# Grouped-query heads of an encoder layer: the scores of two heads issued in one step, instead of one head per step

## The chip, the cores and the metric

The kernel runs on one core of a Trainium2 chip. The metric is the device time of one execution in microseconds (us). The engines are TensorE (PE; its weight loads are a lane of their own, PEld), VectorE (DVE), ScalarE (ACT), GpSimd (POOL) and SyncE (SP, which issues the DMAs). Matmuls write to PSUM, and DVE and ACT read from there.

## The reference

Two pre-norm residual layers over 1024 tokens with 1024 channels. The change lies in the first layer's mixer, in its second half:

```python
# A: differential attention, 4 heads x 2 score maps, v of 128 columns
# B: grouped-query attention, 8 query heads of 64, 2 key/value heads
def gqa_attention(q, k, v):            # q (b,s,2,4,64), k and v (b,s,2,64)
    scale = HEAD_DIM ** -0.5
    def block(qb):                     # 128 queries against all 1024 keys
        s = jnp.einsum('bqgrd,bkgd->bgrqk', qb, k).astype(jnp.float32) * scale
        pr = jax.nn.softmax(s, axis=-1).astype(v.dtype)
        return jnp.einsum('bgrqk,bkgd->bqgrd', pr, v)
    return from_blocks(lax.map(block, to_blocks(q)))
```

The rest (differential attention, neighbourhood attention, the gated ConvFFN, the input embedding, the norms) stays as it is.

## The kernel before

**Precision.** Each float32 operand is split into a high part and a low part of a narrower matmul type, and a product is the sum of three matmuls. For scores the 64 channels of a head fill only half of the 128 rows, so the high and the low part of q are stacked on the 128 rows: one full matmul of 128 rows (line 964, `qs` against `ks`, with the high part of k on both halves) gives two of the three products, and one matmul of 64 rows (line 969, the high half of `qs` against the low part `kl`) gives the third. For heads with even index the high part lies in the lower half of the rows, for odd ones in the upper half (`own`). Scores of 128 queries against 1024 keys fill a PSUM tile S of two banks, so a head needs two matmuls of each kind. There are two S tiles in rotation (`psS`, `bufs=2`), and four more PSUM tiles of one bank each, called b (`psb`), which all other steps share in rotation.

**Work items.** `its` lists 96 items in order: 0 to 31 are (unit, query block) of A, where one item holds both score maps; 32 to 95 are (unit, query block, head j) of B, with 2 units, 8 query blocks, and 4 heads each. An item passes through these stages:

- `qk(n)`: the scores on PE, then the negated row maximum on DVE (line 972).
- `exp(n)`: ACT takes the exponential of S with the row sum as a by-product (line 981), which is issued as two instructions, the activation and a read of the accumulator; the S tile is free after the second.
- `tr(n)`: PE transposes P in two groups of four (line 1007) into two b tiles, and ACT copies each as the high part (line 1017); `tr2(n)`: DVE subtracts to get the low part (line 1029), after which the b tile is free.
- `pv(n)`, for odd j only: 16 matmuls against v for both heads (line 1044); `tail_a`: an ACT copy and a DVE add (lines 1061, 1062); `tail_b`: two small transposes and a DVE multiply (lines 1073, 1078); `place_b`, once in four items: two transposes, an ACT copy and a DVE subtraction (lines 1090, 1093, 1094).

**Order.** Each engine runs its instructions in the order in which the program issues them, so the order in `step(n)` is the order on every queue. For an item of B, step n issues `qk(n)`, `tr(n-2)`, `exp(n)`, `tr2(n-2)`, then `pv(n-3)`, `tail_b(n-4)`, `tail_a(n-3)` and `place_b(n-5)`. So `pv` and `place_b` come in even steps, `tail_b` in odd steps. Between the two halves of a step the main loop puts in other work by hand-written lists of step numbers: one block of the input projection (24 matmuls of 384 columns) at the steps of `PROJ5` (of those from 32 on: 33, 35, 37), one block of the output projection (12 matmuls of 512 columns, lines 175 to 177, and a DVE addition, line 258) at the steps of `GEMM` (57, 59, 61, 63, then every third from 67 to 100), and DVE work left over from the step before (`later`). At the end of a step come the transposes that finish unit 5's queries and keys (`FIN5`: 49, 51, ... 59), those of A's result (`PLACE`: even steps 40 to 54), and a split of the next weight tile (line 164 on ACT, 165 on DVE) where there is room for one.

In A, where an item has two score maps, the same `qk` issues four full matmuls and then four of 64 rows, in the order lower, upper, lower, upper half. In B it issues two full ones and then two of 64 rows, both in the same half:

```python
            for hk in halves:
                for b, ps in zip(bs, e["S"]):
                    o = own[b % 2]
                    nc.tensor.matmul(ps[:, hk], qs[b][o, qc], kl[o, hk], start=False, stop=True)
```

Of the kernel before, what the change touches and what calls it, by code (L numbers as in the profile page):

```python
# [25 lines left out]
P = 128  # L26
S = 1024
# [79 lines left out]
class Kern:  # L107
# [657 lines left out]
    def even(self, W, ready, load, after):  # L765
# [29 lines left out]
        def background(n):  # L795
            while bg and n > 0:
                bg.popleft()()
                n -= 1
# [149 lines left out]
        L, MS = {}, {}  # L948

        def qk(n):  # L950
            u, qt, j = its[n]
            A = u < 4
            if A and qt == 0:
                M[u] = self.u([P, NT, P], F32, "mix")
            qs, ks, kl = st[u]["q"], st[u]["k"], st[u]["kl"]
            e = L[n] = {"P": [], "nm": [], "S": []}
            e["s"] = self.col(2) if j % 2 == 0 else L[n - 1]["s"]
            bs = (0, 1) if A else (j,)
            qc = slice(qt * P, (qt + 1) * P)
            halves = (slice(0, 512), slice(512, 1024))  # L960
            for b in bs:
                ps = self.tS()
                for hk in halves:
                    nc.tensor.matmul(ps[:, hk], qs[b][:, qc], ks[b % 2][:, hk], start=True, stop=False)
                e["S"].append(ps)
# [4 lines that stand above are left out]
            for ps in e["S"]:  # L970
                nm = self.col()
                nc.vector.tensor_reduce(nm, ps, axis=AX.X, op=ALU.max, negate=True)  # L972
                e["nm"].append(nm)

        def exp(n):
            u, qt, j = its[n]
            e = L[n]
            for b, (ps, nm) in enumerate(zip(e.pop("S"), e.pop("nm"))):
                p = self.u([P, S], F32, "P")
                c = b if u < 4 else j % 2  # L980
                nc.scalar.activation(p, ps, AF.Exp, bias=nm, accum_out=e["s"][:, c:c + 1])  # L981
                e["P"].append(p)

        def combine(n):
            u, qt, j = its[n]
            e = L[n]
            if u < 4:
                r = e["r"] = self.col(3)
                s0 = e["s"][:, 0:1]
                nc.vector.reciprocal(r[:, 0:2], e["s"])  # L990
                nc.vector.scalar_tensor_tensor(r[:, 2:3], s0, nlam, r[:, 1:2], op0=ALU.mult, op1=ALU.mult)
                nc.vector.scalar_tensor_tensor(e["P"][0], e["P"][1], r[:, 2:3], e["P"][0],
                                               op0=ALU.mult, op1=ALU.add)
            elif j % 2 == 1:
                r = e["r"] = self.col(2)
                nc.vector.reciprocal(r, e["s"])

        def tr(n):
            u, qt, j = its[n]
            e = L[n]  # L1000
            w = e.pop("P")[0]
            e["T"] = []
            for h in range(2):
                ps = self.tb()
                for b in range(4):
                    kt = 4 * h + b
                    nc.tensor.transpose(ps[:, b * P:(b + 1) * P], w[:, kt * P:(kt + 1) * P], self.ident)
                e["T"].append(ps.rearrange("p (b c) -> p b c", b=4))
            if u < 4:
                e["pt"] = self.u([P, NT, P], F32, "pt")  # L1010
            else:
                if j % 2 == 0:
                    e["pt"] = [[self.u([P, 4, 2, P], F32R, "pt") for _ in range(2)] for _ in range(2)]
                else:
                    e["pt"] = L[n - 1]["pt"]
                for h in range(2):
                    nc.scalar.copy(e["pt"][h][0][:, :, j % 2], e["T"][h])

        def tr2(n):
            u, qt, j = its[n]  # L1020
            e = L[n]
            T = e.pop("T")
            if u < 4:
                nc.scalar.copy(e["pt"][:, 0:4, :], T[0])
                nc.vector.tensor_copy(e["pt"][:, 4:8, :], T[1])
            else:
                for h in range(2):
                    hi, lo = e["pt"][h]
                    nc.vector.tensor_sub(lo[:, :, j % 2], T[h], hi[:, :, j % 2].bitcast(F32))

        def pv(n):
            u, qt, j = its[n]
            e = L[n]
            v = st[u]["v"]
            if u < 4:
                o = e["o"] = self.tb()
                for kt in range(NT):
                    nc.tensor.matmul(o[:, :P], e["pt"][:, kt, :], v[:, kt, :], start=(kt == 0), stop=(kt == NT - 1))
                e.pop("pt")
            elif j % 2 == 1:  # L1040
                o = e["o"] = self.tb()
                for kt in range(NT):
                    for x in range(2):
                        nc.tensor.matmul(o[:, :256], v[:, kt, :], e["pt"][kt // 4][x][:, kt % 4].rearrange("p a b -> p (a b)"),
                                         start=(kt + x == 0), stop=(kt == NT - 1 and x == 1))
                e.pop("pt")
                L[n - 1].pop("pt")

        def tail_a(n):
            u, qt, j = its[n]  # L1050
            e = L[n]
            if u < 4:
                os = e["os"] = self.os()
                ss = self.col()
                xo = M[u][:, qt, :]
                nc.scalar.activation(os[:, :P], e["o"][:, :P], AF.Copy, scale=e["r"][:, 0:1])
                nc.scalar.activation(xo, os[:, :P], AF.Square, accum_out=ss)
                e["rs"] = self.rstd(ss, 1.0 / P)
            elif j % 2 == 1:
                os = e["os"] = self.os()  # L1060
                nc.scalar.copy(os[0:64], e["o"][64:128, :256])
                nc.vector.tensor_add(os[0:64], e["o"][0:64, :256], os[0:64])

        def tail_b(n):
            u, qt, j = its[n]
            e = L[n]
            if u < 4:
                xo = M[u][:, qt, :]
                nc.vector.scalar_tensor_tensor(xo, e["os"][:, :P], e["rs"], gs, op0=ALU.mult, op1=ALU.mult)
            elif j % 2 == 1:  # L1070
                ps = self.tb()
                for b in range(2):
                    nc.tensor.transpose(ps[:, b * 64:b * 64 + 64], e["os"][0:64, b * P:(b + 1) * P],
                                        self.ident[0:64, 0:64])
                if j == 1:
                    MS[u, qt] = self.os()
                xo = MS[u, qt][:, (j // 2) * P:(j // 2 + 1) * P].rearrange("p (h d) -> p h d", h=2)
                nc.vector.tensor_mul(xo, ps[:, :P].rearrange("p (h d) -> p h d", h=2),
                                     e["r"][:, :, None].to_broadcast([P, 2, 64]))
            L.pop(n)  # L1080

        its = [(u, qt, j) for u in range(6) for qt in range(NT) for j in range(1 if u < 4 else 4)]
        N = len(its)
# [17 lines left out]
        def place_b(n):  # L1101
            u, qt, j = its[n]
            ms = MS.pop((u, qt))
            place([ms[:, :P], ms[:, P:]], 2 * u - 4, qt)

        def step(n):

            A = lambda m: 0 <= m < 32
            B = lambda m: 32 <= m < N
            if n < N:  # L1110
                qk(n)
            if A(n - 2):
                pv(n - 2)
            if B(n - 2):
                tr(n - 2)
            if n < N:
                exp(n)
            if B(n - 2):
                tr2(n - 2)
            if A(n - 2):  # L1120
                tail_a(n - 2)
            if A(n - 4):
                tail_b(n - 4)
            yield
            if A(n - 1):
                tr(n - 1)
                tr2(n - 1)
            if n < N:
                combine(n)
            if B(n - 3):  # L1130
                pv(n - 3)
            if B(n - 4):
                tail_b(n - 4)
            if B(n - 3):
                tail_a(n - 3)
            if B(n - 5) and its[n - 5][2] == 3:
                place_b(n - 5)
            background(4 if n < 32 else 2)
            yield
# [35 lines left out]
        for n in range(N + 6):  # L1175
# [4 lines left out]
            s = step(n)  # L1180
# [511 lines left out]
```

## Time and profile before

| | us |
|---|---|
| median of 3 runs | 2802.2 (2801.87 to 2803.43) |
| the profiled execution, its own time | 2802.09 |
| its span | 2800.0 |
| PE busy in the span | 2735.4 (98%) |
| DVE, ACT, POOL busy | 1920.9 (69%), 1402.5 (50%), 669.5 (24%) |
| 128 reductions of line 972 (A and B) | 153.1 busy |
| 128 exponentials of line 981 (A and B) | 143.2 busy |

The profile is one execution, with times from the start of the span. A timeline row gives the start, the time that a run of like instructions took together, the engine, the line, what is written and read, the shapes, the count, and in brackets how long the engine stood idle before it and what ended that. The scores of B run from 369 us to 646 us of the span.

### The profile page before, as it was taken

The page shows a single profiled execution, that of the slowest core. Times are in us where ns is not written, and L with a number is a line of the kernel's source. Part 1 is how long each engine was busy: PE and PEld are TensorE (multiplying, and loading weights), DVE is VectorE, ACT ScalarE, POOL GpSimd, SP SyncE. Part 2 cuts the span into 40 slices and gives each one's busy share as a digit, 9 for nine tenths or more (in the row PEclk, how much of TensorE's full clock was granted, in tenths as well). Part 3 has the DMA queues.
Part 4 walks back from the last instruction along what each step waited for, and adds up shares of the span by engine and source line. Part 5 has one row for each costly group of instructions (what it writes and reads, how often), then busy time and mean ns, then how long its engine had stood idle before and what let it go on. Part 6 is the DMA issues. An engine that isn't in the chain of part 4 may idle for free. (4 is left out here: it accounts for less than half of the span.)

```text
span 2800.0 us, 37183 instructions
## 1 busy us (share of the span) xinstructions
PE 2735.4 (98%) x13776; PEld 2265.7 (81%) x13776; DVE 1920.9 (69%) x3004; ACT 1402.5 (50%) x2727; POOL 669.5 (24%) x756
## 2 busy tenths in 40 slices
PE   8999999999899999999999999999989999999998
PEld 8988877777788888888887878877878888888887
DVE  5677778775677777677645666666667777777753
ACT  4455557563454444534523666666344444453532
POOL 2222751000544444100101001000244444400000
PEclk9999999999999999999999999999999999999999
DMA  4000001100134334833211111124023343472411
GB/s 161 1 24 24 27 8 46 46 16 33 46 135 151 122 126 150 287 119 123 92 68 71 37 58 49 38 71 160 16 97 120 138 151 136 169 274 84 147 46 60
DMA packets 101700, 260.77 MB, mean 93 GB/s; under 512 B 12048, under 2 KB 18320, under 8 KB 101520
## 3 DMA queue, kind: packets, MB, share of 16 engines
q1 hardware_dynamic: 101520, 258.40, 25.9%
q8 instruction: 109, 1.79, 0.3%
q14 instruction: 71, 0.58, 0.1%
HBM read 200.16 MB, written 58.20 MB: 92 GB/s over the span
## 5 line engine op out<-in xcount | busy, mean ns | idle before, releaser
L440 PE MATMUL b<-H,op 128*128 128x512 f32 x2016 | 484.2, 392 | 16.3 <-ACT op L323 13.2
L440 PEld LDWEIGHTS b<-H,op 128*128 128x128 f32 x2016 | 380.4, 189 | 97.0 <-ACT op L323 13.7
L440 PE MATMUL S<-T,op 128*128 128x512 f32 x1512 | 364.3, 390 | 2.2 <-DVE S L464 1.0
L175 PE MATMUL b<-hi,H 128*128 128x512 f32 (+1 forms) x896 | 337.5, 377 | 1.4 <-ACT H L1292 1.4
L440 PEld LDWEIGHTS S<-T,op 128*128 128x128 f32 x1512 | 283.0, 188 | 63.0 <-issue 2.1
L176 PE MATMUL b<-lo,H 128*128 128x512 f32 (+1 forms) x896 | 329.5, 368 | 1.1 <-DVE lo L165 1.1
L177 PE MATMUL b<-hi,H 128*128 128x512 f32 (+1 forms) x896 | 329.9, 368 | 0.4 <-DVE H L1293 0.4
L182 POOL TENSOR_SCALAR col<-col 128x1 f32<-128x1 f32 (+2 forms) x100 | 28.8, 288 | 1254.0 <-ACT xs L222 1072.9
L576 PE MATMUL S<-do,do 128*128 128x512 f32 x924 | 276.6, 390 | 3.5 <-ACT do L323 2.1
L576 PE MATMUL b<-do,do 128*128 128x512 f32 x924 | 275.5, 389 | 0.0
L576 PEld LDWEIGHTS S<-do,do 128*128 128x128 f32 x924 | 172.5, 188 | 41.8 <-ACT do L323 2.9
L576 PEld LDWEIGHTS b<-do,do 128*128 128x128 f32 x924 | 173.5, 188 | 36.2
L981 ACT ACTIVATE P<-S,col 128x1024 f32<-128x1024 f32 x128 | 143.2, 1119 | 111.4 <-DVE col L972 108.9
L324 DVE TENSOR_TENSOR op<-sm,op 128x512 fp32r<-128x512 f32 x168 | 133.2, 793 | 93.2 <-ACT op L323 93.0
L175 PEld LDWEIGHTS b<-hi,H 128*128 128x128 f32 x896 | 169.2, 189 | 22.8 <-ACT H L1292 1.8
L177 PEld LDWEIGHTS b<-hi,H 128*128 128x128 f32 x896 | 168.9, 189 | 21.7 <-DVE H L1293 1.1
L176 PEld LDWEIGHTS b<-lo,H 128*128 128x128 f32 x896 | 169.3, 189 | 21.0 <-DVE lo L165 2.5
L324 DVE TENSOR_TENSOR op<-raw,op 128x512 fp32r<-128x512 f32 x126 | 162.2, 1308 | 2.5 <-ACT op L323 2.1
L972 DVE TENSOR_REDUCE col<-S 128x1 f32<-128x1024 f32 x128 | 153.1, 1216 | 11.1 <-PE S L969 10.1
L175 PE MATMUL b<-H,hi 128*128 128x512 f32 x384 | 157.1, 409 | 0.2 <-ACT H L238 0.2
L177 PE MATMUL b<-H,lo 128*128 128x512 f32 x384 | 150.2, 391 | 0.0
L176 PE MATMUL b<-H,hi 128*128 128x512 f32 x384 | 149.9, 390 | 0.2 <-DVE H L239 0.2
(199 smaller groups left out, 5269.5 us busy)
## 6 DMA issues: line engine op xcount, KB each, us to landing
raw<-in_w_up SPq DMA_DIRECT2D x88, 512.0 KB, 4.8
g_dram<-cv SPq DMA_DIRECT2D x44, 512.0 KB, 2.6
we<-in_w_down SPq DMA_DIRECT2D x44, 512.0 KB, 4.9
wt_dram<-we SPq DMA_DIRECT2D x88, 256.0 KB, 3.1
wd<-wt_dram SPq DMA_DIRECT2D x88, 256.0 KB, 2.9
wd<-in_w_down SPq DMA_DIRECT2D x66, 256.0 KB, 5.3
G<-g_dram SPq DMA_DIRECT2D x64, 256.0 KB, 5.4
raw<-in_w_inc SPq DMA_DIRECT2D x24, 512.0 KB, 3.8
```

The source lines that it names most:

```text
L175: mm(out, st[0], mv[0], start=start, stop=False)
L176: mm(out, st[0], mv[1], start=False, stop=False)
L177: mm(out, st[1], mv[0], start=False, stop=stop)
L182: self.nc.gpsimd.tensor_scalar(r, ss, inv_n, EPS, op0=ALU.mult, op1=ALU.add)
L324: nc.vector.tensor_sub(o[:, 1], src, o[:, 0].bitcast(F32))
L440: mm(out, w[:, x, k], moving(n, y, k), start=(fresh and k + x + y == 0), stop=(k == 3 and x == 1), skip_group_check=True)
L576: mm(out[t], A[:, x, t * P:(t + 1) * P], B[:, y], start=(fresh and k == 0 and x + y == 0), stop=(k == NC - 1 and x == 1), skip_group_check ...
L972: nc.vector.tensor_reduce(nm, ps, axis=AX.X, op=ALU.max, negate=True)
L981: nc.scalar.activation(p, ps, AF.Exp, bias=nm, accum_out=e["s"][:, c:c + 1])
```

## The change

`qk` of an even head now issues the scores of heads j and j+1 of the same key/value head: four full matmuls, then four of 64 rows that alternate between the lower and the upper half, then both row maxima. The entry of item n+1 is filled at the same time, and step n+1 (odd) issues no `qk`. All else keeps its step: the exponential of item n+1 is still issued in step n+1.

```diff
-            e = L[n] = {"P": [], "nm": [], "S": []}
-            e["s"] = self.col(2) if j % 2 == 0 else L[n - 1]["s"]
-            bs = (0, 1) if A else (j,)
+            e = L[n] = {"P": [], "nm": [], "S": [], "s": self.col(2)}
+            bs = (0, 1) if A else (j, j + 1)
...
                 nm = self.col()
                 nc.vector.tensor_reduce(nm, ps, axis=AX.X, op=ALU.max, negate=True)
                 e["nm"].append(nm)
+            if not A:
+                L[n + 1] = {"P": [], "nm": [e["nm"].pop()], "S": [e["S"].pop()], "s": e["s"]}
...
-            if n < N:
+            if n < N and its[n][2] % 2 == 0:
                 qk(n)
```

## The prediction

> **What bounds the kernel now.** I read the page first, then the stage of B by windows, then the timeline of a few of its steps, and last the timeline of A, because A already issues scores in the form that B is to get.
>
> ```profile
> PE 2735.4 (98%) x13776; PEld 2265.7 (81%) x13776; DVE 1920.9 (69%) x3004; ACT 1402.5 (50%) x2727; POOL 669.5 (24%) x756
> ```
>
> PE is the busiest engine by far. By windows, the last 128.7 us of B (busy time of PE, PEld, DVE, ACT and POOL, granted clock, DMA):
>
> ```profile
> 517.30:646.00 128.70, 128.45 (x756) 97.24 (x756) 95.02 (x154) 75.78 (x143) 0.00 (x0) 1.00 0.04 13
> ```
>
> PE has no idle time and full clock, DVE is busy for 74% and ACT for 59%. So a microsecond of PE time taken out is a microsecond gained, unless PE then has to wait for DVE or ACT. Below is a pair of steps of B without other work (74 and 75), and the start of step 76.
>
> ```profile
> 552.70 0.73 PE L964 MATMUL S<-ks,qs 128*128 128x512 f32 x2
> ...
> 554.02 1.09 PE L1007 MATMUL b<-ident,P 128*128 128x128 f32 x8
> ...
> 554.87 2.16 PE L1044 MATMUL b<-pt,v 128*128 128x256 f32 x16
> ...
> 556.86 0.63 PE L964 MATMUL S<-ks,qs 128*128 128x512 f32 x2
> ...
> 558.09 1.09 PE L1007 MATMUL b<-ident,P 128*128 128x128 f32 x8
> 558.19 1.22 DVE L972 TENSOR_REDUCE col<-S 128x1 f32<-128x1024 f32 x1 [0.31 <-PE S L969]
> 558.78 1.07 ACT L1017 CAST pt<-b 128x512 fp32r<-128x512 f32 x2 [1.34 <-PE b L1007]
> 559.11 0.33 PE L1073 MATMUL b<-ident,os 64*128 64x64 f32 x2
> 559.37 0.73 PE L964 MATMUL S<-ks,qs 128*128 128x512 f32 x2
> ...
> 559.74 1.13 ACT L981 ACTIVATE P<-S,col 128x1024 f32<-128x1024 f32 x1
> 560.74 0.21 ACT L981 ACTIVATION_READ_ACCUMULATOR P<-S,col 128x1 f32 x1
> ```
>
> Starts on PE, one after the other, give each part's price: scores 1.32 (552.70 to 554.02) and 1.23, transposes 0.85 before `pv` and 1.02 before line 1073, `pv` 1.99, line 1073 0.26. ACT follows the odd step's transposes: copies 0.69 after their start, the exponential 1.65 after it, and the accumulator is read by 560.95, 2.86 after it. This exponential belongs to the odd step's head, and PE does not wait for it today: the next scores go to the other S tile.
>
> **Term 1, the scores themselves: -25.6 us.** A's four full matmuls and four alternating ones:
>
> ```profile
> 204.27 1.17 PE L964 MATMUL S<-ks,qs 128*128 128x512 f32 x4
> 205.37 0.73 PE L969 MATMUL S<-kl,qs 64*128 64x512 f32 x4
> 206.03 2.05 PE L1038 MATMUL b<-v,pt 128*128 128x128 f32 x16
> ```
>
> Four 64-row matmuls take 0.66 (205.37 to 206.03): two in opposite halves run together. The whole is 1.76. B's pair pays 1.32 + 1.23 = 2.55 for the same, and 0.08 more where `place_b` stands ahead. So 0.80 per pair, and with 32 pairs 25.6. B's matmuls have A's shapes, halves and PSUM tiles, so I take A's price; as the bound from below, without any overlap, the pair saves about 0.1.
>
> **Term 2, the wait for the odd head's S tile: +19.1 us.** After the change `qk(n+2)` needs both S tiles at the start of an even step, and the odd one is free only when the exponential issued in the odd step just before is done. PE, from the start of the odd step's transposes: 1.02 + 0.26, then the even head's two full matmuls (half of 1.10), so 1.83. The tile comes free at 2.86, plus 0.06 from a release to PE's start (a subtraction that ends at 424.62 lets PE start at 424.68):
>
> ```profile
> 423.93 0.69 DVE L1029 TENSOR_TENSOR pt<-b,pt 128x512 fp32r<-128x512 f32 x1 [2.77 <-POOL T L846]
> ...
> 424.68 0.66 PE L1007 MATMUL b<-ident,P 128*128 128x128 f32 x4 [0.84 <-DVE pt L1029]
> ```
>
> So PE waits 2.92 - 1.83 = 1.09. The row maximum, which is now ready earlier, doesn't help: the exponential stands behind the two copies on ACT, and these behind the transposes. Queued behind the waiting PE instruction is everything, since PE is in order. The wait is covered only where other PE work follows the odd step's transposes, as 12 matmuls of the output projection do in step 73, for 2.93:
>
> ```profile
> 549.50 0.48 PE L175 MATMUL b<-hi,H 128*128 128x512 f32 x1
> ...
> 552.11 0.39 PE L177 MATMUL b<-hi,H 128*128 128x512 f32 x1
> ...
> 552.43 0.34 PE L1073 MATMUL b<-ident,os 64*128 64x64 f32 x2
> ```
>
> By the lists of steps, 12 odd steps have such a block (33, 35, 37, 57, 59, 61, 63, 67, 73, 79, 85, 91), step 95 has no scores after it, and 19 are bare: 39 to 55, 65, 69, 71, 75, 77, 81, 83, 87, 89, 93. 19 x 1.09 = 20.7. In four of these (49 to 55) the transposes for unit 5 stand between, for 0.41, and fill that much of the wait: -1.6.
>
> ```profile
> 447.60 0.66 PE L912 MATMUL b<-ident,T 128*128 128x128 f32 x4
> 448.01 0.70 PE L964 MATMUL S<-ks,qs 128*128 128x512 f32 x2
> ```
>
> **Term 3, DVE behind two row maxima: +9 us.** Both maxima now stand ahead of the even step's subtractions on DVE, so `tr2`, the leftover work and `tail_a` come 1.13 to 1.2 later, and they free b tiles. Two maxima one after the other:
>
> ```profile
> 206.49 2.35 DVE L972 TENSOR_REDUCE col<-S 128x1 f32<-128x1024 f32 x2
> ```
>
> From the even step's transposes on, the maxima start at 0.10 and the two subtractions end at about 3.05 and 3.65. PE comes to the odd step's transposes at 2.84, or at 2.98 after `place_b`. There are four b tiles in rotation. Without `place_b` the first half takes a free one and the second comes late enough: nothing. With `place_b` both halves wait for those subtractions, 0.15 each, and the exponential comes 0.25 later: 8 bare pairs, 2.0; in covered pairs 72 and 84 these are PE's own 0.3 each, 0.6. Where A's transposes stand too (`PLACE`) their ACT copy takes its turn: 0.2 in all. The even steps 50 to 60 carry leftover DVE work of unit 5, such as here:
>
> ```profile
> 475.76 0.68 DVE L937 TENSOR_TENSOR kl<-b,ks 64x512 fp32r<-64x512 f32 x1
> ...
> 476.47 0.42 DVE L938 CAST ks<-ks 64x512 fp32r<-64x512 f32 x1
> ```
>
> With a second cast, 1.5, it stands ahead of `tail_a`, which frees the b tile that the projection of step 57 (pair 56) needs: PE is there at 4.1 and the tile at about 5.6, with the 0.3 together 1.7 lost; in pair 60, 1.5; in the bare pairs 50, 52, 54 together 1.6. In pair 34 the projection comes right behind two sets of transposes and needs the first subtraction:
>
> ```profile
> 385.33 1.09 PE L1007 MATMUL b<-ident,P 128*128 128x128 f32 x8
> ...
> 386.65 1.29 DVE L1029 TENSOR_TENSOR pt<-b,pt 128x512 fp32r<-128x512 f32 x2
> ...
> 388.33 0.42 PE L175 MATMUL b<-hi,H 128*128 128x384 f32 x1
> ```
>
> PE would be there at 1.87 instead of 3.0 after the transposes' start, the tile free at 3.1: 1.25 lost. In step 77 the split of a weight tile stands ahead of the copies and so of the exponential, without the scores that hid it: 1.2.
>
> ```profile
> 567.16 1.05 ACT L164 CAST hi<-raw 128x1024 fp32r<-128x1024 f32 x1
> ```
>
> Sum 10.05; the wait of 0.84 that pair 42 already has (row 424.68; POOL sets it) is absorbed, with its follow-up about 1.0. Left: 9. Each of these is a schedule worked out by hand with margins of 0.1 to 0.3, so its bounds are 0 and twice the value.
>
> Nothing is added: matmuls, maxima, exponentials and DMAs keep their counts. The SP and POOL queues keep their order, and the small tiles that are allocated earlier are 24 in rotation, of which a pair uses four.
>
> **Sum.** -25.6 + 19.1 + 9 = +2.5 against the profiled execution's 2802.09, which stands 0.1 below the median: 2804.6.
>
> **The clock.** PE's waits also bear on its clock. Windows of before, the seventh number being the granted clock:
>
> ```profile
> 304.90:308.30 3.40, 1.51 (x12) 1.32 (x12) 3.33 (x9) 1.09 (x2) 2.06 (x2) 1.00 0.00 0
> 308.34:311.75 3.41, 3.41 (x15) 3.41 (x14) 3.41 (x5) 0.04 (x1) 1.63 (x2) 0.50 0.00 0
> ...
> 345.90:349.30 3.40, 1.52 (x11) 1.19 (x10) 3.21 (x7) 3.37 (x9) 1.03 (x3) 1.00 0.00 0
> 366.37:376.60 10.23, 8.74 (x35) 7.47 (x36) 7.93 (x14) 6.49 (x16) 7.01 (x12) 0.50 0.01 2
> ```
>
> With PE busy for 1.51 of 3.40 the clock was halved for the next 3.41, and later once for 10.23; with 1.52 another time it was not. A halved stretch costs PE half of it, 1.7 or 5.1. A bare pair has about 1.4 of waits within 3.4, pairs 52 and 76 over 2. I take none as likeliest. The Trainium skill (TensorE: Matmul & The Clock Gate, The HAM clock gate) says that the throttle comes back after at least one idle window of about 3.4 us. By that rule no wait here reaches it, and the sum stays 2804.6; by the first row above, one or two stretches would make it 2806 to 2815. The trace does not agree with the rule to the letter, since a window that was 44% busy was enough.
>
> **The rivals.**
> - Faster: term 3 doesn't arise, since DVE, busy for 74%, catches up within the even step, and terms 1 and 2 stay: 2802.1 - 6.5 = 2795.6. It decides where term 3 falls below 0.9. For it: margins of tenths; against: pair 34 and pair 56, where the gap is over a microsecond. 0.15.
> - Faster by all: the wait is hidden too, 2776.5. It would need the exponential to end 1.1 sooner after the transposes, and the rows show no slack there. 0.04.
> - Slower, by the clock: PE's new waits halve it, in one long stretch or more: about 2810. It decides from two short stretches or one long one on. 0.15.
> - Slower, by DVE: term 3 is twice as large, since a late subtraction makes the next pair's transposes late as well: 2813.6. For it: DVE in pairs with `PLACE` is the nearest to full. 0.15.
> - It doesn't do what it says, the matmuls in B don't run together: -3 + 28.1 = 2827. Against it stand A's rows. 0.02.
> - The forecast, 2804.6 within the measurement's bound: 0.49.
>
> **How the numbers follow.** A measurement of this kernel tells a change from none at about 0.2%, 5.6 us: 2796.6 to 2807.8. Faster is 0.15 + 0.04, slower 0.15 + 0.15 + 0.02, the same 0.49. The range runs from 2795 (term 3 at nothing) to 2813 (term 3 near its double, or the clock's long stretch): left out are the hidden wait, no overlap, and the ends of both DVE cases, some 0.2. The forecast's own range is 2797 to 2808.
>
> **What would show it.** Right: four 64-row matmuls in B start in twos and take 0.66; PE stands idle in bare odd steps ahead of line 964, released by ACT's line 981, 19 times for about 1.1; two maxima in a row on DVE; waits of line 1007 for line 1029; covered pairs shorter by 0.8 and bare ones longer by 0.3. Wrong: no idle time there (then the exponential is issued or freed earlier than I read), a granted clock under 1 between 384 and 646 us, or a change of length after B.

## The result, and the profile after

The changed kernel takes 2811.5 us (median of 7 runs, 2809.12 to 2814.27) against 2803.21 us before (median of 7). The ratio is 1.0033, with a 95% interval of 1.0022 to 1.0043: slower by 8.3 us. The profiled execution took 2809.12 us, with a span of 2807.3 us. The times of the experiments are medians too (`split_late` ran once), and that of `mixed` has one execution of 7138 us in it, of unknown cause.

The page of the changed kernel, engines' busy time:

```profile
PE 2718.8 (97%) x13776; PEld 2257.3 (80%) x13776; DVE 1914.7 (68%) x3004; ACT 1404.0 (50%) x2727; POOL 669.1 (24%) x756
```

PE does the same 13776 matmuls in 16.6 us less busy time, in a span that is 7.3 us longer. The stage of B shows it more sharply. A pair is named by its even step and lasts until the next pair's first matmul. By windows, pairs 34 to 92 (60 steps), first before and then after (length, then busy time of PE, PEld, DVE, ACT, POOL, and granted clock):

```profile
384.10:637.80 253.70, 252.45 (x1533) 192.62 (x1531) 202.57 (x335) 165.88 (x314) 24.10 (x35) 1.00 0.10 32
```

```profile
381.30:644.30 263.00, 240.64 (x1532) 187.47 (x1530) 200.24 (x335) 164.72 (x314) 24.67 (x36) 0.99 0.09 31
```

PE's busy time falls by 11.8 us, and its idle time goes from 1.25 to 22.4 us; DVE, ACT and POOL do what they did. The stage is 9.3 us longer. (Pair 32, ahead of it, runs partly at half clock, for 10.2 us in the trace of before and for 3.4 us here, and is 2.7 us shorter here.) Who ended PE's idle time is in the list of waits of the changed kernel over the same stage (total, times, longest):

```profile
PE S L963 <- ACT P L982: 13.4, 17, 1.9
...
PE b L1008 <- DVE qs L917: 2.3, 3, 0.8
...
PE b L1008 <- DVE pt L1030: 1.3, 4, 0.7
PE b L1074 <- DVE os L1063: 1.2, 4, 0.6
PE b L175 <- DVE pt L1030: 1.1, 1, 1.1
...
PE b L175 <- DVE qs L917: 0.8, 1, 0.8
...
PE b L175 <- DVE os L1063: 0.6, 1, 0.6
```

The first row is the wait for the odd head's S tile, the others are waits for b tiles that DVE frees. None of them is in the list of before except a wait for line 1029 (1.1 us, twice). The list counts idle time; from start to start, as used further below, the same waits are longer. A bare pair (one whose odd step holds no other work) of the changed kernel, and the start of the next (timeline; line 963 was 964, 968 was 969, 971 was 972, 982 was 981, 1008 was 1007):

```profile
557.60 1.19 PE L963 MATMUL S<-ks,qs 128*128 128x512 f32 x4
...
558.72 0.73 PE L968 MATMUL S<-kl,qs 64*128 64x512 f32 x4
...
559.38 1.09 PE L1008 MATMUL b<-ident,P 128*128 128x128 f32 x8
559.49 2.36 DVE L971 TENSOR_REDUCE col<-S 128x1 f32<-128x1024 f32 x2 [1.10 <-PE S L968]
...
562.23 1.04 PE L1008 MATMUL b<-ident,P 128*128 128x128 f32 x8
...
562.86 1.08 ACT L1018 CAST pt<-b 128x512 fp32r<-128x512 f32 x2
...
563.68 0.73 PE L963 MATMUL S<-ks,qs 128*128 128x512 f32 x2
563.82 1.13 ACT L982 ACTIVATE P<-S,col 128x1024 f32<-128x1024 f32 x1
564.83 0.21 ACT L982 ACTIVATION_READ_ACCUMULATOR P<-S,col 128x1 f32 x1
...
565.10 0.73 PE L963 MATMUL S<-ks,qs 128*128 128x512 f32 x2 [0.68 <-ACT P L982]
```

Scores take 1.78 (557.60 to 559.38), where two heads took 2.55. In the next pair the even head's two full matmuls start at 563.68, and the odd head's have to wait until the exponential's accumulator is read at 565.04; they start at 565.10, 0.06 later. The row maximum for that exponential was done 1.9 us before it (559.49 + 2.36).

### The profile page after: what moved, and what is told of

Its sections match the earlier page's. It is cut to its first block, busy times and chain, and to the rows that moved or that the text cites. A ratio compares the mean times of both kernels' runs of the same rounds, so it can differ in the third digit from the quotient of the medians.

```text
span 2807.3 us, 37171 instructions
## 1 busy us (share of the span) xinstructions
PE 2718.8 (97%) x13776; PEld 2257.3 (80%) x13776; DVE 1914.7 (68%) x3004; ACT 1404.0 (50%) x2727; POOL 669.1 (24%) x756
## 3 DMA queue, kind: packets, MB, share of 16 engines
q8 instruction: 109, 1.79, 0.3%
## 5 line engine op out<-in xcount | busy, mean ns | idle before, releaser
L440 PE MATMUL b<-H,op 128*128 128x512 f32 x2016 | 484.1, 392 | 16.3 <-ACT op L323 13.3
```

Of the source, the lines that this page charges most:

```text
L440: mm(out, w[:, x, k], moving(n, y, k), start=(fresh and k + x + y == 0), stop=(k == 3 and x == 1), skip_group_check=True)
```

## The experiments

Each kernel is the changed one with the edit shown. Each ratio is against runs of the kernel before in the same session, whose medians were 2801.67 to 2802.35.

**The exponential ahead of the copies** (`exp_first`).

```diff
+            first = B(n) and its[n][2] % 2 == 1
+            if first:
+                exp(n)
             if B(n - 2):
                 tr(n - 2)
-            if n < N:
+            if n < N and not first:
                 exp(n)
```

> The changed kernel, with one edit: in the odd steps of B the exponential is issued ahead of the transposes' copies on ScalarE, so the odd head's S tile comes free about 1.1 us sooner. Theory (the loss is PE's waits: 17 us for the odd S tile, about 14 us for b tiles that VectorE frees late, against a saving of 25 us): the 18 waits between an even head's and an odd head's full matmuls shrink from about 1.0 to about 0.1 us each, 15 us in all; the copies of the transposes come 1.1 us later, which may give 0 to 5 us back: 2796 (2793 to 2802). Rival (the loss is the clock, halved by the new waits, and the waits themselves are mostly slack): only the halved stretch near 578 us goes, 2809. Rival (ScalarE has no room): the waits move to the transposes, no change, 2811.

Measured: 2796.73 us, ratio 0.998 (0.9971 to 0.9988). Its waits for S over the stage, and the whole stage by windows:

```profile
PE S L963 <- ACT P L982: 1.8, 2, 0.9
```

```profile
384.50:633.10 248.60, 236.57 (x1526) 185.85 (x1526) 196.42 (x332) 162.91 (x311) 22.78 (x33) 1.00 0.10 33
```

The wait for S goes from 13.4 us in 17 to 1.8 us in 2, and the kernel is 14.8 us shorter than the changed one and faster than before. So taking this wait away is enough to turn slower into faster. PE is still idle for 12.0 us of the stage.

**The odd maximum behind the subtractions** (`max_behind`): `rowmax(n + 1)` is issued in the even step behind `tr2(n - 2)`; `qk` issues the even head's alone.

> The changed kernel, with one edit: the row maximum of the odd head is issued on VectorE behind the even step's two subtractions instead of ahead of them, so that b tiles come free about 1.1 us sooner; the exponentials stay. Theory: pair 34's wait of 1.4 us and the waits of 0.3 us behind place_b in 14 pairs go, and some of those in pairs 38 to 60, 5 to 9 us in all; the 18 waits for the odd S tile (17 us) stay, since the exponential is set by the copies ahead of it: 2804 (2801 to 2807). Rival (VectorE is short of time in these pairs, whatever its order): no change, 2811. Rival (the clock): no change, or 2 us.

Measured: 2810.27 us, ratio 1.0028 (1.0018 to 1.0039). My expectation was wrong. The wait of pair 34 is shorter (its start intervals show 0.34 instead of 1.39), but others grew: the maximum now stands ahead of nothing but the leftover work and `tail_a`, which were late already.

```profile
PE b L1012 <- DVE qs L917: 4.6, 3, 1.6
...
PE b L1078 <- DVE os L1067: 2.4, 5, 0.8
...
PE b L175 <- DVE qs L917: 1.4, 1, 1.4
```

In the changed kernel the same three were 2.3, 1.2 and 0.8. The other part of the miss is the clock. This trace has four stretches of 3.4 us at half clock in the stage, where the changed kernel has one (near 578 us). Two of them, and the stage, by windows:

```profile
409.10:412.40 3.30, 3.30 (x15) 2.55 (x15) 1.50 (x2) 0.63 (x2) 3.30 (x5) 0.50 0.00 0
456.90:460.20 3.30, 3.30 (x11) 1.57 (x10) 1.01 (x4) 1.80 (x4) 0.00 (x0) 0.50 0.78 300
384.50:646.50 262.00, 238.55 (x1522) 188.44 (x1520) 201.02 (x331) 161.97 (x312) 22.04 (x32) 0.97 0.09 31
```

They lie in pairs 40, 50, 52, 54 and 56, which together are 5.3 us longer than in the changed kernel. The other pairs are 4.3 us shorter, 1.6 of it in pair 78, which runs at full clock here. So the move of the maximum gained under 3 us elsewhere, and pairs with a halved clock took it back. All eight runs have a mean clock of 0.991 or 0.992. That the longer waits brought the halving about is likely, since they stand just ahead of it, but not shown.

**Both edits** (`both`).

> The two edits of exp_first and max_behind together: in B's odd steps the exponential ahead of the copies, and the odd head's row maximum behind the even step's subtractions. Theory: most of both kinds of wait goes, 15 and 5 to 9 us: 2789 (2785 to 2796), faster than either kernel, with most of the saving of 25 us kept. The odd maximum then ends about 3.7 us after the even step's transposes start and the exponential about 4.9, which is 0.1 to 0.3 us late for PE. Rival (the clock): 2807 to 2809. Rival (ScalarE's copies now come too late): 2800 or more, with PE's waits at the transposes instead.

Measured: 2801.44 us, ratio 0.9995 (0.9986 to 1.0003), 4.7 us slower than `exp_first` alone. Another miss, and the clock is in it again: the trace has four halved stretches in the stage (near 424, 455, 465 and 476 us), and that of `exp_first` none. The pairs in which they lie (44, 50 to 56) are 5.0 us longer than in `exp_first`. The runs go the same way: the two at a mean clock of 0.993 took 2796.11 and 2799.84 us, and the six at 0.990 or 0.991 took 2801.44 to 2803.68. Pair 42, at full clock, is 2.6 us longer, by a wait for a subtraction on DVE that stands idle for POOL. So this run does not tell how much moving the maximum costs by itself.

**The 64-row matmuls head by head** (`no_alternate`): in B the four are sorted by head, so that two of one half follow one another.

> The changed kernel, with the 64-row matmuls issued head by head, so that two in the same half follow one another, and the second head's behind them; all else stays. Theory (term 1 is real: opposite halves run together): four take about 1.12 us (two starts at 0.34 and 0.32, two at 0.23) instead of 0.66 in each of 32 pairs, and none of it is hidden, because these matmuls come after the wait for S: 15 us more, 2826 (2822 to 2832). Rival (the alternation is worth nothing, the pairing only saves changes between matmuls of 128 and 64 rows): 2811.

Measured: 2809.9 us, ratio 1.0028 (1.0017 to 1.004), the changed kernel's time. My expectation failed. The timeline, the four and what follows:

```profile
561.28 0.73 PE L970 MATMUL S<-kl,qs 64*128 64x512 f32 x4
561.94 0.33 PE L1010 MATMUL b<-ident,P 128*128 128x128 f32 x1
```

They take 0.66 as before, although the program has both of the lower half first. So either the halves don't matter, or PE starts the upper half's matmul ahead of the lower half's second one. The next run tells these apart.

**Both heads in the lower half** (`same_half`).

```diff
-                    o = own[b % 2]
+                    o = own[b % 2 if A else 0]
```

> The changed kernel, with the 64-row matmuls of both heads put on the lower half of the rows. For the odd head this takes the low part of q instead of the high part, so its third product is another one; the work is the same. The run with the matmuls issued head by head took as long as the alternating one, and its trace showed two of them start 6 ns apart all the same. Theory (PE takes matmuls of opposite halves side by side whatever their order, and this is all of term 1): with one half only, the four take about 1.12 us instead of 0.66 in each of 32 pairs, behind the wait for S, 15 us more: 2826 (2821 to 2832). Rival (the saving is in fewer changes between matmuls of 128 and 64 rows, not in the halves): 2811, with four starts evenly 0.23 apart or less.

Measured: 2823.29 us, ratio 1.0078 (1.0065 to 1.0092), 11.8 us more than the changed kernel.

```profile
570.09 1.19 PE L963 MATMUL S<-ks,qs 128*128 128x512 f32 x4
571.21 1.19 PE L968 MATMUL S<-kl,qs 64*128 64x512 f32 x4
572.33 1.09 PE L1008 MATMUL b<-ident,P 128*128 128x128 f32 x8
```

Four in one half take 1.12 us. So the overlap is real, it comes from the two halves, and the order in the program doesn't set it. It is worth 0.46 of the pair's 0.8. The other 0.3 is there without any overlap (2.24 here against 2.55 before). By my reading it is that a pair changes between matmuls of 128 and of 64 rows half as often: starts stand 0.32 to 0.34 apart next to such a change and 0.23 elsewhere. The 11.8 us are less than 32 x 0.46, since in some pairs other waits shrink by it (pair 64 grows by 0.22, pair 70 by 0.48), and a part of them is the clock (its trace has three halved stretches in the stage, and the run at a mean clock of 0.993 took 2821.62).

**Unit 5's finish moved** (`fin_late`): `FIN5 = list(range(52, 64, 2))`.

> The changed kernel, with the six steps that finish unit 5's queries and keys moved from odd steps 49 to 59 to even steps 52 to 62, so that their leftover VectorE work falls in odd steps, which have no row maximum. Theory (the forecast's term 3 was too small because the leftover work, now behind two maxima, holds the b tile of its own transposes and the one of pv): the waits of pairs 48 to 60, about 8 us by the trace, go, and 1.6 us come back where those transposes filled the wait for S: 2805 (2802 to 2808). Rival (VectorE is just too full in these pairs): less than 2 us, 2810.

Measured: 2810.08 us, ratio 1.0029 (1.0017 to 1.0041): the rival's time. By start intervals pairs 48 to 62 take 77.0 us instead of 76.6. Where it went, in step 53:

```profile
463.87 1.04 PE L1008 MATMUL b<-ident,P 128*128 128x128 f32 x8
466.19 0.34 PE L1074 MATMUL b<-ident,os 64*128 64x64 f32 x2 [1.28 <-DVE H L1095]
```

Pairs 48, 50, 58 and 60 became shorter by 0.5 to 1.5, but pairs 52 to 56 and 62 longer; two halved clock stretches lie in them too. In odd steps the leftover work holds up another b tile, since PE has no scores there any more with which to pass the time.

**The two that helped or should have** (`exp_fin`: `exp_first` and `fin_late`).

> The edits of exp_first and fin_late together. Theory: the wait for S stays away, and the waits of pairs 48 to 60, which exp_first still has at about 8 us, go: 2790 (2787 to 2793). In pairs 52 and 54 ScalarE does the copies of unit 5 ahead of the odd exponential, which may cost 0.5 each. Rival: ScalarE's copies in front of the exponential bring the wait for S back in pairs 52 to 62, 2796.

Measured: 2797.35 us, ratio 0.9983 (0.9975 to 0.9992): no gain over `exp_first`, as for `fin_late`. In its trace pairs 48 to 60 take 63.4 us instead of 65.1, and pair 62 takes 10.9 instead of 8.7: the wait went to the next pair.

**A split later** (`split_late`): the `W.pump()` at the end of step 76 is left out.

> The changed kernel, with the split of a weight tile at the end of step 76 left to the end of step 77, that is, behind the odd exponential on ScalarE. Theory: pair 78's wait between the even and the odd head's full matmuls falls from 2.03 to about 1.0 us, and the clock is no longer halved behind it (near 578 us in the profile of the changed kernel), so the pair is about 2 us shorter (12.3 to 10.3 us). Rival (the halving does not come from that wait): the wait falls, and the clock is still halved there.

Pair 78 in the changed kernel, by timeline and windows:

```profile
573.47 0.73 PE L963 MATMUL S<-ks,qs 128*128 128x512 f32 x2
...
576.07 0.73 PE L963 MATMUL S<-ks,qs 128*128 128x512 f32 x2 [1.87 <-ACT P L982]
```

```profile
574.20:577.60 3.40, 1.53 (x9) 0.80 (x9) 2.55 (x6) 1.82 (x4) 0.00 (x0) 0.99 0.01 5
577.65:581.00 3.35, 3.35 (x18) 3.35 (x17) 3.35 (x4) 2.28 (x4) 0.00 (x0) 0.50 0.01 2
```

and with the split later:

```profile
575.30 0.73 PE L963 MATMUL S<-ks,qs 128*128 128x512 f32 x2
576.96 0.73 PE L963 MATMUL S<-ks,qs 128*128 128x512 f32 x2 [0.92 <-ACT P L982]
```

```profile
574.20:577.60 3.40, 2.48 (x15) 1.46 (x13) 2.48 (x6) 3.38 (x7) 0.00 (x0) 1.00 0.41 145
577.65:581.00 3.35, 3.35 (x29) 2.98 (x28) 3.13 (x3) 2.00 (x4) 0.00 (x0) 1.00 0.01 2
```

The wait halves, the clock stays full and the pair goes from 12.34 to 10.56 us, as the theory had it. The wait does not decide the clock alone, though: in `max_behind` pair 78 has the same wait, 2.03, and full clock. The one run took 2810.45 us, and one run cannot tell 2 us from the spread of the changed kernel's; in this execution another stretch, near 425 us, ran at half clock.

**Some pairs back in the old form** (`mixed`, on top of `exp_first`).

```diff
+SINGLE = (34, 50, 52, 54, 56, 58, 60)
...
+            bs = (0, 1) if A else (j, j + 1) if paired(n) else (j,)
...
+            if n < N and not (its[n][2] % 2 == 1 and paired(n)):
                 qk(n)
```

> The kernel of exp_first, with pairs 34 and 50 to 60 back in the form of before (one head per step, exponential behind the copies), and the other 25 pairs in the changed form with the odd exponential first. Theory (a pair gains 0.8 us only where VectorE has time left for both maxima ahead of the rest, and there it keeps it): by the pairs' lengths in the two traces, pairs 50 to 60 go from 57.4 to 53.0 us and pair 34 from 9.06 to 8.49, 4.9 us in all against exp_first's 2796.7: 2792 (2789 to 2795). Rival (VectorE's backlog moves to the pairs at the seams): 2796 or more.

Measured: 2793.09 us, ratio 0.9967 (0.9956 to 0.9979): 8.9 us faster than its runs of before, and 3.6 faster than `exp_first`, of the 4.9 expected. In its trace pairs 50 to 60 take 52.7 us, as expected, and pair 62, at the seam, 0.55 more than in `exp_first`. It is the fastest kernel here.

## Why the prediction was right or wrong

The time, 2811.5, lies in the range of 2795 to 2813, but the likeliest case, 2804.6 and no change, did not come. What came is slower, which had a chance of 0.32. That the range held is in part luck: the third term came out half as large again, or more, and the range was wide enough for it. The sums below are over pairs 34 to 92 of the profiled execution, from start intervals on PE, each less the same interval where nothing waits.

- **Term 1** stood at 0.80 per pair, and the 1.78 against 2.55 above agrees: -24 for these 30 pairs. Its reason was half right, since 0.46 is the overlap, 0.3 comes without it, and the alternating order is worth nothing.
- **Term 2** stood at 19.1, and with step 77's 1.2 from term 3 at 20.3. Measured: 18 waits, 17.3 us together (one of them, 1.0, in pair 94, behind the stage): 0.70 in pair 40, 0.85 to 1.09 after other bare steps without leftover work, 0.38 to 0.63 where unit 5's transposes fill them, and 2.03 in pair 78. The mechanism was right, the size nearly, and every place but one: after step 55 no wait came. `exp_first` takes the wait away and gives 14.8 us back.
- **Term 3** is the step that failed: 9 forecast, about 14 measured (12.4 in waits of over 0.13, 4.2 in those of 0.3 behind `place_b`, less the 2.4 that before had). The length of the stage leaves a little more, 15.5 to 17: it is 9.4 longer by start intervals, and in it lie the -24, 16.3 of term 2 and up to 1.6 of clock. Pair 34 was forecast at 1.25 and shows 1.39. Most of the miss lies in pairs 48 to 60, measured 7.2 longer together. With a saving of 5.6 and 2.5 of waits for S that makes about 10 of this term, where 4.8 was forecast (1.7, 1.5 and 1.6). I had priced the leftover work once per pair, for one b tile, and pair 58 at nothing. It holds two: the tile of its own transposes, which comes up again four tiles on, and the one that `tail_a` frees. A pair without `place_b` was forecast at nothing, but in pair 74 the odd step's transposes take 1.19 where they took 1.02. Step 57, which I worked out by hand, came nearly as said, 1.4 lost with the 0.6 behind `place_b`, where 1.7 was forecast:

```profile
481.11 0.42 DVE L1063 TENSOR_TENSOR os<-b,os 64x256 f32<-64x256 f32 x1
...
481.58 0.50 PE L175 MATMUL b<-hi,H 128*128 128x512 f32 x1 [0.58 <-DVE os L1063]
```

- **The clock**, of which I had taken none as likeliest, adds a little in this kernel. A granted clock under 1 between 384 and 646 us, one of my signs of being wrong, did come: the stretch behind the wait in pair 78. It costs at most 1.6 us, since the even step's transposes and `pv` take 4.41 there and 2.85 in pair 66. Seven runs of the changed kernel spread over 5 us, and their mean granted clock is 0.993 in the three up to 2811.16 and 0.992 in the other four. That these 2 to 3 us are halved stretches is a reading of these figures and not shown by an experiment.
- The rival "term 3 twice as large", 2813.6, was the nearest by mechanism, though its excess lies with the leftover work and not, as I had it, with `PLACE`. The clock's rival, about 2810, is as near in number by chance: one short stretch in the trace is less than it asked for. The rival that the wait is hidden was excluded rightly for this kernel; one move on ACT hides most of the wait, but the time then is 2796.7 and not 2776.5, since term 3 stays. The rival of no overlap fell with `same_half`.

Open: the split of term 3 among its tiles, and what sets off the halved clock. The attempts to move DVE's work (`max_behind` and `fin_late`, each also with `exp_first`) moved waits and gained nothing clear of the spread, three of them with more halved stretches in their traces; only the old form of the pairs gained.

## What to carry to other kernels

When work is pulled forward to share a step, its buffers are taken earlier but freed where they always were: pull the release along (here one exponential ahead of two copies), or the saving turns into a wait. Count too what the moved work was hiding; the scores in the odd step gave DVE 1.3 us per pair in which to free tiles. And form by form: where a schedule has slots of different content, a change that gains in 25 pairs and loses in 7 can be made in the 25. Before a miss of a few microseconds is put down to the schedule, compare the granted clock of the two traces.

## What the runs showed of the hardware

- PE starts 64-row matmuls of opposite halves side by side even where another of the first half stands between them in the program: four take 0.66 us in either order, and 1.12 in one half. The Trainium skill (TensorE: Matmul & The Clock Gate, Part 3: Packing small matmuls — row/col tiling) says that matmuls start strictly in program order; for different halves this trace does not agree. That the built program keeps the kernel's order is taken for granted here; the views of the profile do not show it. So what PE starts need not follow the order in `step(n)` from one half to the other.
- The clock was halved for 3.4 us behind a stretch in which PE was busy for 1.53 of 3.40 us, with one gap of 1.87, and not behind one with 2.48 (`split_late`). But PE's busy time does not settle it: it was not halved behind 1.79 in `max_behind` (first two rows), and halved behind 2.47 in `same_half` (last two), with no gap over 0.93.

```profile
504.60:508.00 3.40, 1.79 (x16) 1.53 (x15) 3.32 (x6) 2.65 (x6) 0.00 (x0) 1.00 0.94 342
508.00:511.40 3.40, 3.40 (x16) 2.53 (x16) 2.93 (x5) 2.63 (x4) 0.00 (x0) 1.00 0.58 196
```

```profile
418.10:421.50 3.40, 2.47 (x10) 1.46 (x10) 2.11 (x5) 1.90 (x4) 3.40 (x7) 1.00 0.02 5
421.55:424.95 3.40, 3.40 (x16) 2.90 (x15) 3.10 (x4) 1.42 (x3) 3.40 (x7) 0.50 0.00 0
```

The Trainium skill (TensorE: Matmul & The Clock Gate, Part 1: The HAM clock gate) asks for an idle window of about 3.4 us; no wait in these stretches is that long, so these traces do not agree.
